# Hybrid decoder layer: a transfer rate of 295 GB/s in the list scheduler, and one kind of FFN weight sum stored whole

## The chip, the cores and the metric

One Trainium2 chip, of which the program uses one core: TensorE (PE), VectorE (DVE), ScalarE (ACT), GpSimd (POOL), SyncE (SP), and 16 DMA engines. The metric is the device time of one execution in microseconds (us). Every transfer of the kernel is issued on SP's queue.

## The reference, cut to what matters

One step of a decoder layer for a prompt of 2048 tokens and 8 decoding tokens, D_MODEL = 1024, all in float32: a mixer (a convolution module beside a gated DeltaNet, one output projection), cross-attention into 256 memory tokens, and a SwiGLU FFN with D_FF = 2816, each behind an RMSNorm and with a residual. The part that the change touches:

```
def swiglu(h, w_gate, w_up, w_down):
    return (jax.nn.silu(h @ w_gate) * (h @ w_up)) @ w_down
```

## The kernel before, in words

The tokens are worked in four blocks of 512 (b = 0 to 3). The mixer runs over two pairs of blocks first (about 0 to 740 us for the projections, on to some 1200 us with the first two attentions); then come FFN 0, attention 2, FFN 1, attention 3, FFN 2, FFN 3. The 8 decoding tokens ride along.

**Weights.** TensorE multiplies float32 data as two parts. A weight tile of 128 x 512 float32 (256 KB) is loaded into a raw tile (`rpool`, 11 of them, `NRAW`) and split into a tile `w` (`wpool`, 6 slots, `NW`): ScalarE copies it, rounded, into the first half, and GpSimd or VectorE writes raw minus that half into the second (`WS.split`, lines 951 to 975). A product then takes three matmuls for each 128 x 128 piece: high by high, high by low, low by high (`three`).

**FFN with sums.** Gate and up projections of one f (128 of the 2816 columns, 22 f in all) are computed by a scheme of Winograd's kind: seven products in place of eight, on blocks of half the rows and half the tokens (`ffn`, `product`). Three of the products take a plain half of w_gate or w_up (Q1, Q2, P4), four take a sum of such halves: P5, P6, Q3 and Q7, which are kinds 0 to 3 (`PROD`, line 803). Kind 3 is gate half 0 plus up half 0. The sums of f = 0 to 7 are made late in the mixer's second pair (`SUMS_AT`, about 490 to 740 us), those of f = 8 to 21 in FFN 0. Each sum is added into a raw tile, split into a w slot like any weight, and that slot, both halves, 512 KB, is stored to the DRAM tensor `sums`, 22 x 4 stores (line 972). For f = 0 to 7 the split slot is used for nothing else; for f = 8 to 21 it also feeds FFN 0's product. All other uses load the 512 KB from `sums` straight into a w slot, without a raw tile (line 957): 8 x 4 in FFN 0 and 22 x 4 in each of FFN 1 to 3, 296 loads.

**Order of the weights.** `Plan` (line 726 on) is the list of all weight tiles in the order of use. An entry either names a raw tile (a load, a sum of two raws) or, with -1, a direct load into w. `WS.pump` loads and splits ahead in that order: raws up to 4 entries ahead (8 in an FFN) and while one of the 11 raw tiles is free, splits while one of the 6 slots is free.

**Order of the instructions.** Two models of time decide it. First, while the program is generated, class `Clock` with `dma` (lines 600 to 608, 360 bytes per ns) decides which lane of work goes on next; this gives the program's order. Second, `Tape` records every operation and `Tape.order` lists them anew for all five engines: it takes a cost for each (`Tape.cost`), and lets the operation go next whose engine and inputs are free first, by a key from the program's order. A transfer costs SP 450 ns; its data start 1100 ns after the issue or when the transfers before it have ended, take size / 360 ns (line 190), and count as there 0.91 to 0.985 us later, according to the engine that reads them (`LAT`):

```
if e == "sp":
    clock[e] = s + 450
    dma_at = max(dma_at, s + 1100) + ns
    fin = dma_at
```

The engines' queues are then in that order, and each engine takes its own in order, waiting where an input is not there.

Of the kernel before, what the change touches and what calls it, by code (L numbers as in the profile page):

```python
# [8 lines left out]
F32 = mybir.dt.float32  # L9
# [5 lines left out]
P = 128  # L15
# [3 lines left out]
TB = 512  # L19
# [13 lines left out]
NF = DFF // P  # L33
# [69 lines left out]
def elems(ap):  # L103
    n = 1
    for x in ap.shape[1:]:
        n *= x
    return n
# [37 lines left out]
class Tape:  # L145
# [28 lines left out]
    def cost(self, eng, op, args, kw, outs, ins):  # L174

        n = max(elems(a) for a in outs + ins) if ins else elems(outs[0])
        psum_in = any(a.name in self.psum for a in ins)
        if eng == "pe":
            m = elems(args[1])
            n = elems(args[2])  # L180
            if op == "transpose":
                return max(n, m) * 0.835 + 3, False, None
            if args[1].dtype == F32:
                return 2 * (max(max(m, 64) * 0.835, 2 * n * 0.4492) + 3), False, None
            return max(max(m, 64) * 0.835, (n if n >= 256 else 4 * n) * 0.4492) + 3, False, None
        if eng == "sp":
            size = 4
            for x in outs[0].shape:
                size *= x
            return max(size / 360.0, 90.0), False, None  # L190
        if eng == "act":
            ptr = len(ins) - 1
            return 0.834 * n + (50 if psum_in else 94) + 93 * ptr + (92 if "accum_out" in kw else 0), False, SETS.get(kw.get("func"))
        big = sum(a.name not in self.psum and elems(a) > 1 for a in ins)
        if eng == "dve":
            ptr = any(hasattr(kw.get(k), "shape") for k in ("scalar", "scalar1"))
            half = op in ("tensor_copy", "tensor_scalar") and not psum_in
            return 68 + (61 if ptr else 0) + n * (6.2 if op == "reciprocal" else 0.525 if half else 1.042), big > 1, None
        if kw.get("op") == ALU.pow:
            return 280 + 180 * n, True, None  # L200
        if op in ("memset", "affine_select"):
            return 40 + 0.85 * n, False, None
        return 135 + n * (2.14 if op == "tensor_tensor" else 3.4), True, None
# [388 lines left out]
def hybrid_step(ctx: ExitStack, tc: tile.TileContext, i: dict, o: list):  # L592
# [7 lines left out]
    def dma(out, in_, after=0.0):  # L600
        SP.dma_start(out=out, in_=in_)
        n = 4
        for x in out.shape:
            n *= x
        C.at["sp"] = max(C.at["sp"] + 60, C.when([in_]), after)
        C.at["dma"] = max(C.at["dma"], C.at["sp"] + 1100) + max(n / 360.0, 60.0)
        C.ready[out.name] = max(C.ready.get(out.name, 0.0), C.at["dma"] + 1650)
        C.used[in_.name] = max(C.used.get(in_.name, 0.0), C.at["dma"])
# [21 lines left out]
    dram = tape.pool(ctx.enter_context(tc.tile_pool(name="dram", bufs=1, space=bass.MemoryType.DRAM)), 1)  # L630
# [4 lines left out]
    def nm(s):  # L635
        uid[0] += 1
        return f"{s}_{uid[0]}"
# [114 lines left out]
    plan = Plan()  # L752
# [49 lines left out]

    PROD = {"P5": 0, "P6": 1, "Q3": 2, "Q7": 3}

    def ffn_key(st, f):
        if st in PROD:
            return ("sums", "c", f, PROD[st])
        w, half = {"Q1": ("w_gate", 0), "Q2": ("w_gate", 1), "P4": ("w_up", 1)}[st]
        return (w, "c", f, half)

    def ffn_plan(b):
        at = {}
        for st, f, *j in ffn_steps(b):
            if st == "down":
                plan.append(("w_down", "d", f, j[0]))
            elif st == "dec":
                plan.append((f, "r", j[0] % KC, j[0] // KC * TB))
            elif b or any(f in fs for fs in SUMS_AT.values()):
                plan.append(ffn_key(st, f), -1 if st in PROD else None)
            else:  # L820
                if st == "Q1":
                    plan.append(ffn_key(st, f))
                    at["Q1", f] = plan.raw_of[-1]
                    continue
                if st == "P5":
                    u1, u0 = (plan.raw("dma", "w_up", "c", f, half) for half in (1, 0))
                    g0, g1 = at["Q1", f], plan.raw("dma", "w_gate", "c", f, 1)
                    s1 = plan.raw("sum", u0, u1, f, 0)
                    s2 = plan.raw("sum", s1, g0, f, 1)
                    at = {**at, "Q2": g1, "P4": u1, "P5": s1, "P6": s2}  # L830
                    at["Q3"] = plan.raw("sum", g1, s2, f, 2)
                    at["Q7"] = plan.raw("sum", g0, u0, f, 3)
                plan.append(ffn_key(st, f), at[st])
# [22 lines left out]
    for pair in PAIRS:  # L856
        for st in STEPS:
            k = int(st[1])
# [28 lines left out]
    for b in range(NB):  # L887
        ffn_plan(b)
        if b + 2 < NB:
            out_plan(b + 2)  # L890
            att_plan(b + 2)
        elif b + 1 < NB:
            plan.extend(("w_down", "d", g, j) for g in range(NG - HOLD, NG) for j in range(KC // 2))
    plan.extend(("w_down", "d", NG - 1, j) for j in range(KC // 2))

    wsrc = dict(i)

    class WS:
# [28 lines left out]
        def load(self):  # L927
            j = self.ld
            how, *what = plan.raws[j]
            r = rpool.tile([P, TB], F32, tag="raw", name=nm("raw"))  # L930
            fr = self.done.get(j - NRAW, 0.0)
            if how == "sum":
                x, y, f, k = what
                self.engine(2600.0).tensor_tensor(out=r, in0=self.raw[x], in1=self.raw[y], op=ALU.add)
                self.used(x)
                self.used(y)
            else:
                w, kind, a, b_ = what
                src = wsrc[w]
                if kind in "cd":  # L940
                    dma(r, src[a, b_], fr)
                elif kind == "q":
                    k0 = b_[0]
                    src = src[0, k0 * P : (k0 + 4) * P, a * P : (a + 1) * P].rearrange("(k p) c -> p k c", p=P)
                    dma(r.rearrange("p (k c) -> p k c", k=4), src, fr)
                else:
                    dma(r, src[0, a * P : (a + 1) * P, b_ : b_ + TB], fr)
            self.raw[j] = r
            self.ld += 1

        def split(self):
            j = self.sp
            k = plan.raw_of[j]
            t = wpool.tile([P, 2, TB], F32R, tag="w", name=nm("w"))
            if k < 0:
                _, _, f, n = plan[j]
                dma(t.bitcast(F32), wsrc["sums"][f, n], self.ends.get(j - NW, 0.0))
                self.tiles[j] = t
                self.sp += 1
                return  # L960
            r = self.raw[k]
            A.activation(out=t[:, 0, :], in_=r, func=AF.Copy)
            if self.pool_lo == "near":
                eng = self.engine()
            elif self.pool_lo is None:
                eng = G if max(C.at["pool"], S.vt) + 600 < max(C.at["dve"], S.vt) else V
            else:
                eng = G if (self.pool_lo or any(c[0] is not None for c in convs)) and j > 9 else V
            eng.tensor_tensor(out=t[:, 1, :], in0=r, in1=t[:, 0, :].bitcast(F32), op=ALU.subtract)
            if plan[j][0] == "sums":  # L970
                _, _, f, n = plan[j]
                dma(wsrc["sums"][f, n], t.bitcast(F32))
            self.tiles[j] = t
            self.sp += 1
            self.used(k)
# [1001 lines left out]
    zd = {(h, b): dram.tile([P, TB], F32, tag=f"z{h}_{b}", name=f"z{h}_{b}") for h in range(H) for b in range(NB)}  # L1977
    udone, cat_done, sdone, zdone = set(), set(), set(), set()
    wsrc["wk"] = dram.tile([1, D, D], F32, tag="wk", name="wk")
    wsrc["sums"] = dram.tile([NF, 4, P, 2, TB], F32, tag="sums", name="sums")  # L1980
    xpark = dram.tile([NB - 1, KC, P, TB], F32, tag="xpark", name="xpark")
    wsrc["vp"] = dram.tile([1, D, D], F32, tag="vp", name="vp")
# [91 lines left out]
    for pair in PAIRS:  # L2074
# [3 lines left out]
        for st in STEPS:  # L2078
# [8 lines left out]
            k = int(st[1])  # L2087
# [342 lines left out]
    def norm_res(xs, done, gain, res, rows_too, split=True):  # L2430

        yield from norm_raw(
            [(lambda k=k: k in done, lambda k=k: xs()[k]) for k in range(KC)], gain, res, True, split, rows_too,
            spare=0,
        )
# [455 lines left out]
```

## Time and profile before

| | |
|---|---|
| runs of the kernel before | 2984.43, 2984.06, 2978.11 us (median 2984.06) |
| the profiled execution, own time | 2980.41 us |
| its span, first to last instruction | 2978.7 us |
| mean granted clock of TensorE | 0.996 |
| PE, DVE, ACT, POOL busy | 98%, 66%, 46%, 50% of the span |
| moved by DMA | 593.89 MB, 199 GB/s on the mean |

Shares are of the span. TensorE's matmuls are pipelined, so that "busy" is time in which at least one is under way. Tiles are named without numbers: `w<-raw` is the split's copy, `w<-raw,w` its subtraction, `w<-sums` a load of a stored sum, `fx`, `fy`, `fz` the banks of the seven products, `dn` those of the down projection. Almost every instruction carries line 469, the line that issues the recorded operations, so groups are told apart by tile names.

### The profile page before, as it was taken

Reading aid. Unit: us, or ns where it says so; the run is one execution under the profiler, and the core shown is the slowest. Engines: PE = TensorE matmul, PEld = TensorE weight load, DVE = VectorE, ACT = ScalarE, POOL = GpSimd, SP = SyncE. Lnnn points to the kernel's source line nnn. Section 1 sums busy time; section 2 is a strip of 40 time slices with the busy share of each in tenths; the row PEclk is TensorE's granted clock in tenths of the full one; section 3 lists DMA queues with packets and bytes.
Section 4 is the critical chain, followed back from the end, with each engine's and each line's share of the span. In section 5 each row is a group of like instructions: output and inputs, shape, how many; then the busy total and the mean of one; then the engine's idle time right before and its main releaser. Section 6 shows DMA issues by size and latency. Waiting matters only on the chain.

```text
span 2978.7 us, 53399 instructions
## 1 busy us (share of the span) xinstructions
PE 2922.9 (98%) x18972; PEld 2601.6 (87%) x18972; DVE 1975.7 (66%) x3973; ACT 1373.8 (46%) x2854; POOL 1478.0 (50%) x1407
## 2 busy tenths in 40 slices
PE   9999999999999998999999999999999999999998
PEld 7999878887888887999988789988888999999997
DVE  8757798987684867957689874433775444664345
ACT  6543556455764545635554553333453232333233
POOL 3544545776656454548875124445503444344444
PEclk9999999999999999999999999999999999999999
DMA  6533435877773435766778767867526666676663
GB/s 213 158 96 106 130 110 163 262 239 255 225 224 112 140 101 162 253 190 222 256 251 273 252 210 244 262 227 241 176 93 233 208 223 214 213 245 216 223 220 134
DMA packets 361962, 593.89 MB, mean 199 GB/s; under 512 B 54016, under 2 KB 148544, under 8 KB 361680
## 3 DMA queue, kind: packets, MB, share of 16 engines
q1 hardware_dynamic: 361696, 590.47, 61.4%
q8 instruction: 151, 2.47, 0.3%
q14 instruction: 115, 0.94, 0.1%
HBM read 476.65 MB, written 114.27 MB: 198 GB/s over the span
## 4 chain that ended last, share of the span: by engine, by line
PE 76%; DVE 7%; issue 5%; DMA 5%; POOL 5%; ACT 2%; SPq 0%; POOLq 0%; DVEq 0%; ACTq 0%
PE dn L469 14%; PE hd L469 11%; PE fy L469 11%; PE rg L469 9%; PE fx L469 7%; PE fz L469 7%; PE sc L469 5%; POOL w L469 3%; DVE cacc L469 3%; PE pu L469 2%; PE glua L469 2%; PE glub L469 2%; DMA w<-sums 1%; PE pch L469 1%; PE po L469 1%
## 5 line engine op out<-in xcount | busy, mean ns | idle before, releaser
L469 POOL TENSOR_TENSOR w<-raw,w 128x512 fp32r<-128x512 f32 x709 | 957.4, 1361 | 877.7 <-ACT w L469 830.3
L469 ACT ACTIVATE w<-raw 128x512 fp32r<-128x512 f32 x912 | 568.6, 631 | 827.7 <-PE fx L469 175.0
L469 PE MATMUL dn<-ff,w 128*128 128x512 f32 (+2 forms) x2688 | 514.2, 347 | 0.8 <-DVE ffs L469 0.6
L469 PEld LDWEIGHTS dn<-ff,w 128*128 128x128 f32 x2688 | 422.8, 188 | 61.5 <-issue 0.8
L469 PE MATMUL fy<-op,w 128*128 128x256 f32 (+1 forms) x3168 | 426.5, 282 | 3.6 <-DMA w<-sums 3.5
L469 PEld LDWEIGHTS fy<-op,w 128*128 128x128 f32 x3168 | 398.6, 188 | 8.9 <-DVE ffu L469 2.8
L469 PE MATMUL hd<-hT,w 128*128 128x512 f32 (+2 forms) x1920 | 397.7, 357 | 8.2 <-ACT w L469 6.0
L469 DVE SCALAR_TENSOR_TENSOR cacc<-cu,cw,cacc 128x512 f32<-128x512 f32 x480 | 359.5, 749 | 16.1 <-ACT cacc L469 8.2
L469 PEld LDWEIGHTS hd<-hT,w 128*128 128x128 f32 x1920 | 304.3, 189 | 52.5 <-ACT w L469 6.8
L469 DVE TENSOR_TENSOR x<-dn,x 128x512 f32<-128x512 f32 (+1 forms) x448 | 254.4, 572 | 139.4 <-PE dn L469 136.1
L469 PE MATMUL fz<-op,w 128*128 128x256 f32 (+1 forms) x2112 | 287.4, 282 | 0.2 <-DMA w<-sums 0.2
L469 PE MATMUL fx<-op,w 128*128 128x256 f32 (+1 forms) x2112 | 284.7, 282 | 0.3
L469 PEld LDWEIGHTS fx<-op,w 128*128 128x128 f32 x2112 | 267.2, 189 | 6.9 <-issue 1.2
L469 PEld LDWEIGHTS fz<-op,w 128*128 128x128 f32 x2112 | 265.3, 188 | 2.2 <-issue 1.3
L469 POOL TENSOR_TENSOR sqj<-sqj,sqj 128x512 f32<-128x512 f32 (+1 forms) x98 | 134.1, 1368 | 265.5 <-ACT sqj L469 263.3
L469 DVE TENSOR_TENSOR w<-raw,w 128x512 fp32r<-128x512 f32 x203 | 180.0, 892 | 69.4 <-ACT w L469 66.0
L469 PE MATMUL rg<-pT,w 128*128 128x512 f32 x768 | 191.5, 401 | 8.1 <-ACT cres L469 7.9
L469 PE MATMUL sc<-w,hT 128*128 128x512 f32 x768 | 189.4, 398 | 2.4 <-DVE w L469 1.3
L469 PE MATMUL rg<-catS,w 128*128 128x512 f32 (+1 forms) x960 | 188.2, 352 | 1.8 <-ACT jn L469 1.7
L469 DVE TENSOR_TENSOR ffu<-fy,ffu 128x256 f32<-128x256 f32 (+1 forms) x176 | 74.4, 423 | 167.2 <-PE fy L469 167.2
L469 PEld LDWEIGHTS rg<-catS,w 128*128 128x128 f32 x960 | 154.4, 188 | 27.0 <-ACT jn L469 2.5
L469 PEld LDWEIGHTS rg<-pT,w 128*128 128x128 f32 x768 | 142.0, 190 | 40.7 <-ACT cres L469 8.3
(378 smaller groups left out, 4101.2 us busy)
## 6 DMA issues: line engine op xcount, KB each, us to landing
w<-sums SPq DMA_DIRECT2D x296, 512.0 KB, 4.5
raw<-in_w_gate_dram SPq DMA_DIRECT2D x192, 256.0 KB, 3.3
sums<-w SPq DMA_DIRECT2D x88, 512.0 KB, 4.1
raw<-in_w_down_dram SPq DMA_DIRECT2D x176, 256.0 KB, 3.0
raw<-in_w_up_dram SPq DMA_DIRECT2D x118, 256.0 KB, 2.9
raw<-in_w_in_dram SPq DMA_DIRECT2D x96, 256.0 KB, 3.1
raw<-in_w_out_dram SPq DMA_DIRECT2D x64, 256.0 KB, 4.3
raw<-wk SPq DMA_DIRECT2D x64, 256.0 KB, 2.9
```

The costliest lines, as they stand in the source:

```text
L469: fn(*args, **kw)
```

## The change

The list scheduler's rate for transfers goes from 360 to 295 GB/s (`Tape.cost` alone; `dma` in line 606 keeps 360). Kind 3 (`WHOLE = (3,)`, product Q7) is kept in a DRAM tensor of its own, `sums1`, as the float32 sum: it is stored from the raw tile, 256 KB, and each later use loads those 256 KB into a raw tile and splits them like a plain weight. Kinds 0 to 2 stay as they are, and so do the additions and first splits of kind 3.

```diff
--- before.py
+++ after.py
@@ -187,7 +187,7 @@
             size = 4
             for x in outs[0].shape:
                 size *= x
-            return max(size / 360.0, 90.0), False, None
+            return max(size / 295.0, 90.0), False, None
         if eng == "act":
             ptr = len(ins) - 1
             return 0.834 * n + (50 if psum_in else 94) + 93 * ptr + (92 if "accum_out" in kw else 0), False, SETS.get(kw.get("func"))
@@ -802,6 +802,9 @@
 
     PROD = {"P5": 0, "P6": 1, "Q3": 2, "Q7": 3}
 
+
+    WHOLE = (3,)
+
     def ffn_key(st, f):
         if st in PROD:
             return ("sums", "c", f, PROD[st])
@@ -816,7 +819,12 @@
             elif st == "dec":
                 plan.append((f, "r", j[0] % KC, j[0] // KC * TB))
             elif b or any(f in fs for fs in SUMS_AT.values()):
-                plan.append(ffn_key(st, f), -1 if st in PROD else None)
+                if st not in PROD:
+                    plan.append(ffn_key(st, f))
+                elif PROD[st] in WHOLE:
+                    plan.append(ffn_key(st, f), plan.raw("dma", "sums1", "u", f, WHOLE.index(PROD[st])))
+                else:
+                    plan.append(ffn_key(st, f), -1)
             else:
                 if st == "Q1":
                     plan.append(ffn_key(st, f))
@@ -937,7 +945,7 @@
             else:
                 w, kind, a, b_ = what
                 src = wsrc[w]
-                if kind in "cd":
+                if kind in "cdu":
                     dma(r, src[a, b_], fr)
                 elif kind == "q":
                     k0 = b_[0]
@@ -967,9 +975,12 @@
             else:
                 eng = G if (self.pool_lo or any(c[0] is not None for c in convs)) and j > 9 else V
             eng.tensor_tensor(out=t[:, 1, :], in0=r, in1=t[:, 0, :].bitcast(F32), op=ALU.subtract)
-            if plan[j][0] == "sums":
+            if plan[j][0] == "sums" and plan.raws[k][0] == "sum":
                 _, _, f, n = plan[j]
-                dma(wsrc["sums"][f, n], t.bitcast(F32))
+                if n in WHOLE:
+                    dma(wsrc["sums1"][f, WHOLE.index(n)], r)
+                else:
+                    dma(wsrc["sums"][f, n], t.bitcast(F32))
             self.tiles[j] = t
             self.sp += 1
             self.used(k)
@@ -1977,6 +1988,7 @@
     zd = {(h, b): dram.tile([P, TB], F32, tag=f"z{h}_{b}", name=f"z{h}_{b}") for h in range(H) for b in range(NB)}
     udone, cat_done, sdone, zdone = set(), set(), set(), set()
     wsrc["wk"] = dram.tile([1, D, D], F32, tag="wk", name="wk")
+    wsrc["sums1"] = dram.tile([NF, len(WHOLE), P, TB], F32, tag="sums1", name="sums1")
     wsrc["sums"] = dram.tile([NF, 4, P, 2, TB], F32, tag="sums", name="sums")
     xpark = dram.tile([NB - 1, KC, P, TB], F32, tag="xpark", name="xpark")
     wsrc["vp"] = dram.tile([1, D, D], F32, tag="vp", name="vp")
```

## Rows read from the trace of the kernel before

**Rows 1.** The page: busy time of each engine, and all DMA traffic.

```profile
PE 2922.9 (98%) x18972; PEld 2601.6 (87%) x18972; DVE 1975.7 (66%) x3973; ACT 1373.8 (46%) x2854; POOL 1478.0 (50%) x1407
...
DMA packets 361962, 593.89 MB, mean 199 GB/s; under 512 B 54016, under 2 KB 148544, under 8 KB 361680
```

**Rows 2.** Windows by stage: length, each engine's busy us (instructions), clock, DMA share, GB/s.

```profile
540.00:740.00 200.00, 197.76 (x989) 161.21 (x988) 168.32 (x291) 109.23 (x218) 147.84 (x146) 0.99 0.79 258
740.00:1200.00 460.00, 438.71 (x2568) 374.26 (x2566) 333.86 (x647) 247.96 (x564) 249.50 (x242) 0.99 0.53 164
...
1380.00:1620.00 240.00, 238.86 (x1628) 215.72 (x1627) 188.70 (x278) 123.54 (x252) 187.52 (x145) 1.00 0.75 254
...
1740.00:2100.00 360.00, 357.13 (x2440) 325.34 (x2439) 164.19 (x290) 132.00 (x249) 162.94 (x124) 1.00 0.76 248
...
2640.00:2960.00 320.00, 319.39 (x2239) 298.13 (x2238) 133.99 (x235) 101.05 (x196) 141.97 (x107) 1.00 0.65 212
```

**Rows 3.** Who PE waited for, whole span: us in total, times, longest us.

```profile
PE rg L469 <- ACT cres L469: 7.9, 1, 7.9
...
PE vp L469 <- ACT jn L469: 3.8, 4, 2.0
PE fy L469 <- DMA w<-sums: 3.5, 6, 1.0
...
PE pu L469 <- DMA Tm<-zt: 2.9, 2, 2.0
PE hd L469 <- POOL w L469: 2.2, 1, 2.2
PE lnp L469 <- DMA lnx<-cvT: 2.1, 1, 2.1
PE wk L469 <- ACT jn L469: 1.9, 1, 1.9
...
PE fz L469 <- DMA w<-sums: 0.2, 1, 0.2
```

**Rows 4.** The page: DMA issues, count, KB each, median us from issue to landing.

```profile
w<-sums SPq DMA_DIRECT2D x296, 512.0 KB, 4.5
raw<-in_w_gate_dram SPq DMA_DIRECT2D x192, 256.0 KB, 3.3
sums<-w SPq DMA_DIRECT2D x88, 512.0 KB, 4.1
```

**Rows 5.** Groups, 1740 to 2960 us, POOL, then ACT: busy us, mean ns, idle before.

```profile
L469 POOL TENSOR_TENSOR w<-raw,w 128x512 fp32r<-128x512 f32 x339 | 458.0, 1364 | 547.5 <-ACT w L469 512.1 <-DMA w<-sums 24.8 <-DMA out_dram<-x 2.8
...
L469 ACT ACTIVATE w<-raw 128x512 fp32r<-128x512 f32 x397 | 248.8, 630 | 424.6 <-PE fx L469 155.4 <-PE fy L469 76.6 <-PE fz L469 62.7
```

**Rows 6.** Windows of 10 us inside 540 to 740 us, columns as in rows 2.

```profile
560.00:570.00 10.00, 10.00 (x56) 8.47 (x55) 10.00 (x17) 7.00 (x15) 7.23 (x8) 1.00 0.93 326
570.00:580.00 10.00, 10.00 (x50) 7.96 (x48) 8.10 (x15) 3.71 (x7) 8.14 (x10) 1.00 1.03 329
...
670.00:680.00 10.00, 10.00 (x47) 8.15 (x46) 8.12 (x21) 4.24 (x7) 6.91 (x11) 1.00 1.04 375
690.00:700.00 10.00, 7.76 (x39) 6.20 (x38) 9.75 (x16) 3.62 (x8) 6.53 (x6) 0.99 0.99 331
```

**Rows 7.** DMA issues, whole span: a store of 256 KB, columns as in rows 4.

```profile
xpark<-x SPq DMA_DIRECT2D x24, 256.0 KB, 3.8
```

**Rows 8.** Who SP's queue waited for, 1380 to 1620 us, columns as in rows 3.

```profile
SPq L469 <- POOL w L469: 55.1, 38, 6.8
SPq L469 <- DVE w L469: 26.0, 20, 3.9
...
SPq L469 <- POOL raw L469: 11.7, 9, 3.2
```

**Rows 9.** Who PE waited for, 1380 to 1620 us: all of it.

```profile
PE pu L469 <- DMA Tm<-zt: 0.9, 1, 0.9
PE dn L469 <- ACT ffs L469: 0.2, 1, 0.2
```

## The prediction

> **What bounds the kernel now.** I read the page's busy time first: TensorE is busy 2922.9 of 2978.7 us, so whatever the change does to the other engines, only 55.8 us of TensorE idle can be won [rows 1]. The same rows give the bytes moved, 593.89 MB. Next the stages, as windows: the idle of TensorE (window minus PE busy) is 2.2 us in the crowded mixer stretch 540 to 740, 21.3 us in 740 to 1200, 1.1 us in 1380 to 1620 (second half of the first FFN block, where sums are made), 2.9 us in 1740 to 2100 (second block) and 0.6 us in 2640 to 2960 (last block) [rows 2]. The reader is to see that the stages that carry the sums are nearly full of matmuls, and that the idle sits in the mixer's second half, which reads no sums at all. Third, who ends TensorE's waits: the sums' loads end 3.5 + 0.2 us of them in seven waits, none over 1.0 us; two other transfers 2.9 and 2.1 us; tiles that go out to DRAM and come back as weights (jn) 3.8 and 1.9 us; a weight split on GpSimd 2.2 us; and one stop of 7.9 us belongs to an ACT instruction [rows 3]. So the kernel is bound by TensorE, and the change is worth what it does to a few short waits and to the order in which every engine's instructions stand.
>
> **Part one, kind 3 kept whole.** There are 296 loads and 88 stores of 512 KB, a quarter of each of kind 3: 74 loads and 22 stores become 256 KB [rows 4]. That is 96 x 0.262 = 25.2 MB less, 4.2% of all traffic [rows 1]. In 1740 to 2100 it is 22 x 0.262 = 5.8 MB of 89. Such a load is now sent for a raw tile (11 of them, loaded ahead) and not for a slot of w.
>
> What it is worth: 0.262 MB at that stage's 248 GB/s is 1.06 us [rows 2]. A sums load that follows one of kind 3 in the transfers' queue lands sooner by up to this, and the longest of the waits to be removed is 1.0 us [rows 3]. I take all of them: 3.7 us. The bounds are 3.7 us gained, and 3.7 us more where the extra raw loads stand in SP's queue ahead of a sums load and wait for a raw tile.
>
> What it adds: 74 copies on ScalarE at 630 ns = 46.6 us and 74 subtractions, on GpSimd at 1364 ns = 100.9 us [rows 5]. In a block of 22 that is 14 and 30 us; in 1740 to 2100 ScalarE is busy 132 and GpSimd 163 of 360 us [rows 2], so both have room and I cost this at nothing. The work that hides it is the matmuls of the other five slots of w. The new wait is ScalarE's, for a slot that TensorE frees; behind it in its queue stand the copies and Silu of the product banks, which TensorE needs back. From the free slot to a ready weight it takes 0.63 + 1.36 = 2.0 us, against 4.5 us for the transfer it replaces [rows 4, 5], so the weight is not late. Without that cover each of 74 uses could hold TensorE for up to 2.0 us, 148 us; the slots' present 397 splits do not, since no wait on them shows in the FFN [rows 3], so I do not carry this into the range.
>
> The eight f of the mixer stage still split kind 3, though nothing reads that split; its slot no longer waits for a store. The eight additions and splits there stay as they are: no time.
>
> **Part two, 295 in place of 360.** It moves no byte. It changes the reckoned end of every transfer, so the order that the list writes out for all five engines, SP's and GpSimd's queues too. A transfer is reckoned at 1.1 us to start, its bytes, and 0.93 us until TensorE may use it: for 256 KB 1.1 + 0.73 + 0.93 = 2.76 us before and 2.92 after, for 512 KB 3.49 before and 3.81 after. Measured medians from issue to landing are 3.3 and 4.5 us [rows 4]. So the list believed transfers 0.54 and 1.0 us early, and put what reads them too early into in-order queues; the change mends 0.16 and 0.32 us, about a third of either.
>
> What it acts on: the two waits on other transfers (5.0 us), those behind weights that were written and read back (5.7 us) and the split behind crowded transfers (2.2 us), together 12.9 us [rows 3]. Bounds: all of it gone, 12.9 us; with the 7.9 us stop gone as well, which is an accident of order in ScalarE's queue, 20.8 us; on the other side a rewritten list can put as much of it elsewhere, so 12.9 us more, since no row excludes that. I take the third that the mended part stands for, 4.3 us, nearest to the landings, which are the only rows that measure the reckoned quantity.
>
> The Trainium skill ("DMA: Bandwidth & Descriptors", section "Where 436 GB/s comes from") speaks against this part: it puts the limit between HBM and SBUF at about 358 GB/s for a core. By that the old figure was the right one. The trace agrees for bursts: where the engines are full they moved 329 and 375 GB/s in 10 us [rows 6]. It does not for a single transfer, whose landing is nearer to the new figure [rows 4]. By the rule, part two would bring nothing, or the loss in rival two.
>
> **Sum.** -3.7 - 4.3 = -8.0 us against the profiled execution's 2980.4 us (span 2978.7 and 1.7 around it): 2972.4. The median of the runs shown is 3.7 us above that execution, so 2976.1; I say 2976.
>
> **Rivals.** *One: hidden anyway.* The sums' waits are seven in a span of 2979 us, the last block loses 0.6 us in all [rows 2, 3], and program order itself still comes from the old 360, since the second clock (line 606) keeps it; 0.16 us on a transfer then moves few neighbours. In this the change hardly does what it says, as only order that the transfers decide can move. For it: FFN stages already full. Against: 21.3 us of idle in 740 to 1200, which a new order must touch [rows 2]. Time: 2984 less at most 3.7, between 2980 and 2987.
>
> *Two: the old rate was right.* Where transfers really run at over 295 GB/s, the list now reckons its transfer queue fuller than it is and sets readers late. In the mixer stretch four windows of 10 us exceed it, at 326, 329, 375 and 331 GB/s [rows 6]: reckoned at 295 their bytes take 1.05, 1.15, 2.71 and 1.22 us longer, 6.1 us. If all of this reaches TensorE and nothing is won, 2990. It decides where such a reader is alone in TensorE's queue; against it stands that these stages have other matmuls to put in front.
>
> *Three, slower: the raw tiles in the first FFN block.* There kind 3 of 14 f is stored from its raw tile, which until now came free after copy and subtraction, 2.0 us [rows 5]. It will be held by a 256 KB store; such a store lands in 3.8 us [rows 7]. That is 1.8 us longer for 14 tiles, 25 us. SP there already waits for raw tiles: 55.1, 26.0 and 11.7 us on splits and sums in 1380 to 1620 [rows 8], so later tiles mean later loads, and behind them in SP's queue stand the decode rows' weights and w_down. For a loss: GpSimd is busy 187.5 of 240 us there [rows 2]. Against: TensorE waits for nothing but 1.1 us in it [rows 9], so the loads are ahead by some unknown measure. It decides when that lead is under 1.8 us; half of the price, 12 us, gives 2996.
>
> **How the numbers follow.** A difference of 0.2%, 6 us, is about what a measurement of this kernel can tell from none. Forecast with its better neighbours (the 7.9 us stop gone as well: 2968, all bounds together: 2960): 0.45, its own range 2958 to 2978. Rival one 0.32. Rival two 0.09, rival three 0.14, both slower. So faster 0.45, same 0.32, slower 0.23. The range goes from the bounds of the forecast, 24.5 us gained at the most (2959.6), with 3 us for the spread of runs, to rival three at half price: 2957 to 2996.
>
> **What would show it.** Right in part one: 222 loads and 66 stores of sums at 512 KB, 74 loads of the new tensor, 569 MB in all, and no wait on sums above some tenths of a us in 1740 to 2100. Right in part two: the waits on Tm, lnx and jn shorter by a third in 740 to 1380 and no new one of their size. Rival three would show as TensorE waits on a split between 1380 and 1620, rival two as idle in 540 to 740 above 2.2 us. The forecast is wrong if TensorE's idle stays within 3 us of 55.8, or if a new stop of the kind of the 7.9 us one opens: a rewritten order can make one anywhere, and no row of the old order tells where.

## The result, and the profile after

The changed kernel is faster: 2963.71 us against 2984.16, medians of four runs each, ratio 0.9932 (95% interval 0.9915 to 0.9949). A second measurement beside the experiments gave 0.9930 (0.9910 to 0.9950). The forecast had 2976, and 8 us where 20 were gained. The profiled execution took 2965.75 us, 14.7 us less than the one of before.

The page of the changed kernel, the lines that answer to [rows 1], then the three groups that carry the splits (columns as in [rows 5]):

```profile
PE 2926.8 (99%) x18972; PEld 2605.1 (88%) x18972; DVE 1969.6 (66%) x3978; ACT 1413.4 (48%) x2925; POOL 1581.4 (53%) x1476
...
DMA packets 361963, 568.72 MB, mean 192 GB/s; under 512 B 54016, under 2 KB 148544, under 8 KB 361680
...
L469 POOL TENSOR_TENSOR w<-raw,w 128x512 fp32r<-128x512 f32 x778 | 1053.4, 1364 | 813.7 <-ACT w L469 754.9
L469 ACT ACTIVATE w<-raw 128x512 fp32r<-128x512 f32 x986 | 613.3, 631 | 832.6 <-PE dn L469 177.3
...
L469 DVE TENSOR_TENSOR w<-raw,w 128x512 fp32r<-128x512 f32 x208 | 182.3, 882 | 75.0 <-ACT w L469 73.4
```

Idle of TensorE fell from 55.8 to 2964.0 - 2926.8 = 37.2 us, 18.6 us less; the span fell by 14.7 only, because the same matmuls were busy for 3.9 us longer, in an execution whose mean granted clock was 0.994 where that of before had 0.996. The traffic is 25.2 MB less, as reckoned. The subtractions were 709 on GpSimd and 203 on VectorE, and are 74 more in all, mostly on GpSimd, at the same 1364 ns.

DMA issues of the changed kernel (columns as in [rows 4]): 74 loads and 22 stores of 256 KB have taken the place of as many of 512 KB.

```profile
w<-sums SPq DMA_DIRECT2D x222, 512.0 KB, 4.4
...
sums<-w SPq DMA_DIRECT2D x66, 512.0 KB, 3.7
...
raw<-sums SPq DMA_DIRECT2D x74, 256.0 KB, 2.8
...
sums<-raw SPq DMA_DIRECT2D x22, 256.0 KB, 3.7
```

Who TensorE waited for in the changed kernel (whole span; total, times, longest), the lines to hold against [rows 3]:

```profile
PE hd L469 <- ACT w L469: 6.3, 2, 5.7
...
PE pu L469 <- DMA Tm<-zt: 1.9, 3, 0.9
...
PE vp L469 <- ACT jn L469: 0.7, 1, 0.7
...
PE fz L469 <- DMA w<-sums: 0.2, 1, 0.2
```

The largest one left is mostly the start's (5.7 of 6.3 us). The waits on sums went from 3.7 to 0.2 us, and no row names ACT cres any more, on which TensorE stood for 7.9 us. Windows of the changed kernel (columns as in [rows 2]) say where idle went:

```profile
540.00:740.00 200.00, 197.27 (x1004) 160.45 (x1003) 176.62 (x315) 112.09 (x221) 152.36 (x151) 1.00 0.76 246
740.00:1200.00 460.00, 453.13 (x2662) 389.44 (x2662) 305.70 (x611) 255.36 (x587) 253.13 (x241) 0.99 0.54 170
...
1380.00:1620.00 240.00, 238.26 (x1584) 212.28 (x1584) 190.43 (x276) 121.25 (x249) 182.66 (x139) 1.00 0.71 241
...
1740.00:2100.00 360.00, 358.86 (x2475) 329.46 (x2475) 172.91 (x289) 146.54 (x275) 198.84 (x148) 1.00 0.72 232
```

In 740 to 1200 it is 6.9 us where it was 21.3 [rows 2]. No matmul in it uses a sum until FFN 0 begins (at 1189.7 us before and 1175.3 us after); to say that the stretch reads no sums, as the prediction did, goes too far, since seven of their loads are issued in its last 22 us in the kernel before. The last block was as good as full before.

**Three stages.** Windows at fixed times mix stages that have moved, so I cut the span at two matmuls instead: the first of attention 0's output product of the mixer (`rg<-catS,w`) and the same of attention 2. Work that moves between an attention and FFN 0 stays within one stage this way. For the kernel before these are the first starts in two windows of that tile, 740 to 1300 and 1400 to 1800 us:

```profile
L469 PE MATMUL rg<-catS,w x576: 277/284/496, 850.4 to 1078.8; 128*128 128x256 f32 x64, 128*128 128x264 f32 x64, 128*128 128x512 f32 x64
...
L469 PE MATMUL rg<-catS,w x192: 388/392/481, 1611.2 to 1656.7; 128*128 128x512 f32 x192
```

So: 850.4 us to attention 0 (mixer, memory weights), 760.8 to attention 2 (attentions 0 and 1, FFN 0), 1367.5 for the rest (attentions 2 and 3, FFN 1 to 3). In the changed kernel 852.1, 751.1 and 1360.8: +1.7, -9.7, -6.7. The middle one is itself a difference: up to FFN 0's first product it fell from 339.3 to 323.2 us, and FFN 0 grew from 421.5 to 427.9 us, with TensorE idle for 7.0 us of it where it was 4.7 (before, then changed; columns as in [rows 2]):

```profile
1189.70:1611.20 421.50, 416.79 (x2977) 382.14 (x2976) 320.11 (x568) 218.17 (x485) 288.39 (x253) 1.00 0.73 240
```

```profile
1175.30:1603.20 427.90, 420.88 (x2981) 384.33 (x2980) 339.77 (x602) 224.66 (x500) 311.16 (x274) 0.99 0.68 226
```

Two gains of different kinds, then, and the runs below show that neither comes, in the main, from the part to which the prediction gave it.

### The profile page after: what moved, and what is told of

Its sections match the earlier page's. It is cut to its first block, busy times and chain, and to the rows that moved or that the text cites. A ratio compares the mean times of both kernels' runs of the same rounds, so it can differ in the third digit from the quotient of the medians.

```text
span 2964.0 us, 53559 instructions
## 1 busy us (share of the span) xinstructions
PE 2926.8 (99%) x18972; PEld 2605.1 (88%) x18972; DVE 1969.6 (66%) x3978; ACT 1413.4 (48%) x2925; POOL 1581.4 (53%) x1476
## 4 chain that ended last, share of the span: by engine, by line
PE 81%; DVE 7%; DMA 5%; POOL 3%; issue 2%; ACT 1%; SPq 0%; POOLq 0%; DVEq 0%; ACTq 0%
PE dn L469 16%; PE fy L469 12%; PE hd L469 10%; PE fz L469 8%; PE fx L469 8%; PE rg L469 7%; PE sc L469 5%; PE glua L469 2%; PE pu L469 2%; PE glub L469 2%; DVE cacc L469 1%; PE pch L469 1%; PE mkv L469 1%; POOL w L469 1%; PE po L469 1%
## 5 line engine op out<-in xcount | busy, mean ns | idle before, releaser
L469 POOL TENSOR_TENSOR w<-raw,w 128x512 fp32r<-128x512 f32 x778 | 1053.4, 1364 | 813.7 <-ACT w L469 754.9
L469 ACT ACTIVATE w<-raw 128x512 fp32r<-128x512 f32 x986 | 613.3, 631 | 832.6 <-PE dn L469 177.3
L469 PE MATMUL rg<-catS,w 128*128 128x512 f32 (+2 forms) x960 | 188.2, 352 | 0.0
L469 PEld LDWEIGHTS sc<-w,hT 128*128 128x128 f32 x768 | 141.5, 188 | 34.6 <-DVE w L469 1.4
```

Of the source, the lines that this page charges most:

```text
L469: fn(*args, **kw)
```

## The experiments

All profiles in one table, us; the ratio is to the kernel before, run beside it. "Sums" is TensorE's wait on loads of sums as the profile lists it, "P3" the time from attention 1's first `rg<-pT,w` to FFN 0's first `fx<-op,w`, its output product, all worked out from the first starts in each trace. "Program order" is the order in which the first clock has the operations recorded; kernels with the same word share it:

```
kernel             program  list   ratio   interval         to att 0  to att 2  rest    P3    sums
                   order    rate
before             old      360    1                        850.4     760.8     1367.5  59.8  3.7
rate 362           old      362    1.0045  1.0026 - 1.0064  864.0     764.0     1373.1  60.0  6.3
start 1640         old      360    0.9978  0.9968 - 0.9987  841.1     764.2     1363.8  59.8  2.4
rate 330           old      330    0.9982  0.9970 - 0.9993  851.5     760.7     1362.5  59.8  2.1
rate 295 alone     old      295    0.9963  0.9953 - 0.9973  852.3     762.2     1360.0  59.8  1.1
kind 3 alone       new      360    0.9980  0.9970 - 0.9989  857.3     749.2     1366.6  50.3  1.5
kind 3, rate 300   new      300    0.9965  0.9952 - 0.9978  853.3     759.0     1362.5  50.1  1.6
the change         new      295    0.9932  0.9915 - 0.9949  852.1     751.1     1360.8  50.1  0.2
the change again   new      295    0.9930  0.9910 - 0.9950  851.3     750.4     1360.2  50.1  1.2
kind 3, rate 290   new      290    0.9937  0.9918 - 0.9957  848.4     751.4     1361.7  50.2  0.0
kind 3, rate 270   new      270    0.9998  0.9987 - 1.0008  859.0     758.3     1360.5  50.1  0.0
kinds 0 and 3      third    295    1.0018  1.0007 - 1.0028  860.0     761.1     1360.2  52.4  0.0
room for cres      fourth   360    1.0022  1.0008 - 1.0035  849.4     767.4     1366.1  51.3  2.5
first clock 295    fifth    360    1.0087  1.0066 - 1.0108  883.4     756.9     1368.3  52.6  5.2
```

One profile is one execution, and those of the rate alone, of rate 300, of rate 362 and of first clock 295 were 6, 9, 11 and 6 us above the medians of their kernels; the two of the change agree within 1 us in each stage.

**The two parts apart.** The rate alone:

```diff
-            return max(size / 360.0, 90.0), False, None
+            return max(size / 295.0, 90.0), False, None
```

> The rate 295 alone, all four kinds of sums still stored split. Theory A (the rate mends the order, kind 3 mends the sums' waits, the two add up): the stretch from the first matmul of attention 0 to the first of FFN 0 falls from 339.3 us to about 323 as in the changed kernel, the sums' waits stay near 3.7 us, FFN 0 stays at 421 us and does not grow to 428; time about 2968 us. Theory B (the order is a draw: any new figure deals the stops out anew): no relation to 323 us; time anywhere from 2965 to 3000 us. Theory C (kind 3 alone brought it): 2984 us, the stop of 7.9 us still there.

2970.05 against 2981.25 us. Its waits on TensorE:

```profile
PE rg L469 <- ACT cres L469: 7.9, 1, 7.9
PE vp L469 <- ACT jn L469: 6.0, 6, 2.1
...
PE wk L469 <- ACT jn L469: 4.6, 3, 2.2
...
PE lnp L469 <- DMA lnx<-cvT: 2.0, 1, 2.0
...
PE pu L469 <- DMA Tm<-zt: 1.4, 2, 1.2
...
PE fy L469 <- DMA w<-sums: 0.8, 1, 0.8
...
PE fz L469 <- DMA w<-sums: 0.3, 1, 0.3
```

The time came out as theory A had it, and its reasons did not: the stop is still there, to the tenth of a us, and the waits on sums, which A left to kind 3, are down from 3.7 to 1.1 us without it. From attention 0 to FFN 0 it took 339.1 us and not 323. The gain that the stages show is in the rest, 7.5 us; 2.6 us of it are the waits on sums, and what the others are no run parts. Kind 3 alone, the changed kernel with 360:

```diff
-            return max(size / 295.0, 90.0), False, None
+            return max(size / 360.0, 90.0), False, None
```

> Kind 3 stored whole, rate still 360. Theory A: the sums' waits fall from 3.7 us to under 1, FFN 1 to 3 are 4 to 5 us shorter, the stop of 7.9 us near 1153 us stays, FFN 0 may grow by up to 6 us; time 2978 to 2986 us. Theory B: 2965 to 3000 us, with the large stops at other places. Theory C: about 2964 us.

2975.25 us: below A's band of 2978 to 2986 and inside B's, and by stages again the wrong way round for A. No row of its waits names cres; attention 0 to attention 2 is 11.6 us shorter, the rest only 0.9. The rest in windows, for the kernel before, the rate alone and kind 3 alone (columns as in [rows 2]):

```profile
1611.20:2978.70 1367.50, 1348.64 (x9169) 1235.88 (x9168) 741.24 (x1554) 507.57 (x977) 534.85 (x404) 1.00 0.66 214
```

```profile
1614.50:2974.50 1360.00, 1346.32 (x9169) 1235.18 (x9167) 742.24 (x1554) 507.47 (x976) 536.94 (x404) 1.00 0.67 215
```

```profile
1606.50:2973.15 1366.65, 1350.42 (x9169) 1237.71 (x9167) 753.53 (x1561) 544.95 (x1043) 618.28 (x463) 0.99 0.63 201
```

By TensorE's idle time kind 3 alone does a little more than the 0.9 us say: 18.9 us before, 16.2 with it, 13.7 with the rate alone. Its matmuls were busy for longer in this one execution, at a granted clock of 0.99. Theory C falls with this as well. The two ratios, 0.9963 and 0.9980, multiply to 0.9943; with an interval of 0.0010 to either side on each that reaches the 0.9930 and 0.9932 of both together.

**What the stop was.** TensorE and ScalarE of the kernel before, in order of time:

```profile
1139.12 6.51 PE L469 MATMUL rg<-pT,w 128*128 128x512 f32 x27
1153.52 3.78 PE L469 MATMUL rg<-pT,w 128*128 128x512 f32 x8 [7.89 <-ACT cres L469]
```

```profile
1148.55 1.30 ACT L469 ACTIVATE op<-tt 128x512 fp32r<-128x512 f32 x2 [0.37 <-DVE tt L469]
1151.69 0.42 ACT L469 ACTIVATE op<-xn 128x256 fp32r<-128x256 f32 x1 [1.84 <-DVE xn L469]
1152.36 0.63 ACT L469 ACTIVATE op<-xn 128x512 fp32r<-128x512 f32 x1 [0.25 <-DVE xn L469]
1152.89 0.58 ACT L469 ACTIVATE cres<-cacc 128x512 f32<-128x512 f32 x1
```

Attention 1's output product needs four accumulator banks. In the list of the kernel before three of them get their matmuls in turn, and the fourth comes after them alone, in the bank in which the convolution accumulated (`cacc`). That bank is emptied by the copy `cres<-cacc`, and TensorE goes on 0.05 us after that copy's end. The stop costs more than its 7.9 us: in it the granted clock fell to 0.50, 1.2 GHz, from 1150.4 us on, and it was full again at 1157.2 us, when TensorE was back at work. The window of that stretch (columns as in [rows 2]):

```profile
1150.40:1157.20 6.80, 3.68 (x9) 2.90 (x10) 6.60 (x14) 5.26 (x13) 0.08 (x1) 0.50 0.75 223
```

So eight matmuls behind the stop took 3.78 us, where nine of the same kind in the changed kernel, below, took 2.33. In ScalarE's queue twelve operand copies of FFN 0 (`op`) stand directly ahead of it from 1138.6 us on, and they wait for VectorE in turn. In the changed kernel all four banks get their matmuls in turn, and none of them is the convolution's: that one is emptied earlier and taken at once for the next channels, while the product's matmuls run.

```profile
1131.89 0.60 ACT L469 ACTIVATE cres<-cacc 128x512 f32<-128x512 f32 x1
...
1134.12 0.81 ACT L469 ACTIVATE cacc<-cu,vcol,cw 128x512 f32<-128x512 f32 x1
```

```profile
1136.04 5.79 PE L469 MATMUL rg<-pT,w 128*128 128x512 f32 x24
1141.66 0.60 PE L469 MATMUL pod<-ident,osc 128*128 128x128 f32 x4
1142.02 2.33 PE L469 MATMUL rg<-pT,w 128*128 128x512 f32 x9
```

Which bank a product takes and how early the copy is called is settled in the program's order, by the first clock. Kind 3 changes that order, since its entries now take raw tiles; the list's rate does not, and every kernel of the table with the old program order has P3 at 59.8 to 60.0 us, whatever its rate. Two kernels tried it without kind 3. First, the copy asks for less room, in the second pair of blocks:

```diff
-        yield ("t2", 1 + RES)
+        yield ("t2", 1 + (RES if b < 2 else 0))
         res = t2("cres")
```

> The kernel before; the copy that empties the convolution's accumulator bank asks for one free tile in place of six, in the second pair of blocks, so that it stands earlier in the program's order. No byte and no rate changes. Theory D (the 7.9 us stop is a bank: the fourth accumulator of attention 1's output product takes the convolution's bank, which that copy frees from behind a dozen FFN-norm copies in ScalarE's queue; kind 3 removed it only by another program order): the stop is gone and the last product of attention 1 falls from 59.6 us to about 50, time about 2971 us (8 to 12 us less). Theory E (the stop went with the transfers of kind 3): the stop stays, 2981 us.

P3 fell to 51.3 us and the stop went, so D holds on its place. On its time it does not: 1.0022. The new order opened another stop of the same length in FFN 0, a small DeltaNet matmul behind ScalarE's `lny`:

```profile
PE pu L469 <- ACT lny L469: 7.9, 1, 7.9
```

Second, another program order with no other edit:

```diff
-        C.at["dma"] = max(C.at["dma"], C.at["sp"] + 1100) + max(n / 360.0, 60.0)
+        C.at["dma"] = max(C.at["dma"], C.at["sp"] + 1100) + max(n / 295.0, 60.0)
```

> The kernel before with 295 in place of 360 in the first clock alone (line 606), so another program order with the same bytes and the old list rate. Theory D: its four accumulators stand together in the list, so no stop of 7.9 us, and the last product of attention 1 takes about 50 us; the sums' waits stay at 3 to 4 us; other stops move by some us either way, time 2965 to 2980 us. Theory E: the stop stays.

P3 52.6 us, no stop on cres, and yet 0.87% slower, outside what D allowed: 33 us more before attention 0. So the bytes of kind 3 were not what took the stop away (E falls), and a program order that avoids it can cost more elsewhere.

**Is the rate's gain in its truth?** Other rates, and another start, with either program order.

```diff
-            return max(size / 360.0, 90.0), False, None
+            return max(size / 362.0, 90.0), False, None
```

> The kernel before with a list rate of 362 in place of 360, nearly nothing. Theory A: within 3 us of the kernel before. Theory B: differs by more than 4 us, one way or the other; its stops at other places.

Half a percent in the rate cost 0.45%, 9.4 us by the medians. Its profile, itself 11 us above its median, loses 13.6 us before attention 0: 7.6 us of idle, and 6.0 us in which TensorE was busy for longer at a granted clock of 0.99 in place of 1.00. Waits of that kernel, whole span:

```profile
PE lnq L469 <- DVE lnx L469: 9.0, 3, 4.2
PE rg L469 <- ACT cres L469: 7.9, 1, 7.9
...
PE fy L469 <- DMA w<-sums: 5.7, 6, 2.2
```

That is theory B: in the mixer, where many chains share the engines' queues, a new list can deal the stops anew.

```diff
-                dma_at = max(dma_at, s + 1100) + ns
+                dma_at = max(dma_at, s + 1640) + ns
```

> The kernel before, list rate 360, but a transfer's data reckoned to start 1640 ns after its issue in place of 1100, which mends the whole 0.54 us by which a 256 KB landing was reckoned short. Theory A (truer landings make a better order): at least as good as 295 alone, 2970 us or less. Theory B (any new order deals the stops anew): no relation, 2968 to 2992 us.

0.9978, 2973.17 us: short of A's bound and inside B's, with waits on sums of 2.4 us. By the landings that the prediction took, it mends that of a 256 KB transfer wholly and that of a 512 KB one by half, and is worth rather less than the rate 295, which mends a third of both (0.9963; the intervals just overlap).

```diff
-            return max(size / 360.0, 90.0), False, None
+            return max(size / 330.0, 90.0), False, None
```

> The kernel before with a list rate of 330. Theory A (a truer rate is a better order throughout): between the runs at 360 and at 295, 2972 to 2981 us. Theory B (in the mixer the order is a draw): mixer and first attention differ from both by 5 us or more, 2965 to 2995 us. Theory F (B for the mixer, but in FFN 1 to 3 a slower rate takes the sums' waits away for good): FFN 1 to 3 between 1069 and 1075 us with waits on sums of 1 to 4 us, whatever the mixer does; last product of attention 1 at 59.8 us in all three, since the program's order is the old one.

2974.69 us; by its total A and F are alike, by stages F's figures came true: FFN 1 to 3 (FFN 1 from its first `fx<-op,w` to attention 3, FFN 2 and 3 from theirs to the end) took 1071.9 us where the kernel before took 1075.0, waits on sums 2.1, P3 59.8. B's did not: to attention 0 and from there to FFN 0 this kernel is within 1.4 us of both its neighbours, 360 and 295. So not every new list deals the mixer anew; 362 did. With kind 3 whole, and so the new program order, 300, 290 and 270 in place of 295, and the change itself once more:

```diff
-            return max(size / 295.0, 90.0), False, None
+            return max(size / 300.0, 90.0), False, None
```

> The changed kernel with 300 in place of 295. Theory A: a rate 1.7% off is as good, within 4 us of the changed kernel, 2960 to 2968 us, no stop over 4 us on TensorE before the tail. Theory B: another order, differing by 6 us or more one way or the other, with stops that neither kernel had.

> The changed kernel with 290 in place of 295. Theory A: within 4 us of the changed kernel, 2960 to 2968 us. Theory B: differs by 6 us or more from the changed kernel or from the run at 300.

> The changed kernel with a list rate of 270, slower than any 60 us stretch of the trace moved on the mean but two. Theory A (an optimum near the true landing): slower than at 295 by 3 to 10 us. Theory F: FFN 1 to 3 as at 295 within 2 us, no waits on sums; mixer and FFN 0 drawn anew, 2955 to 2980 us.

> The changed kernel once more, as the base of the runs beside it. Every theory: 0.990 to 0.996 of the kernel before; the last product of attention 1 at 50 us, sums' waits under 0.5 us.

The change again: 2961.04 us, as expected in ratio and P3, with 1.2 us of waits on sums where under 0.5 was expected. 300 gave 2967.58 us and 0.9965, against 0.9930 and 0.9932 for 295. By the ratios, each with its own runs of before, that is some 10 us, by the medians 4 to 7. Its median lies inside A's band and its profile has no stop over 4 us but the start's, as A had it; too little to settle it. 290 is as good as 295 (2962.35 us). 270 loses all that was gained (2980.91 us), and not in the rest, where it is as good as any (1360.5), as F had it: it loses 7 to 8 us in each of the two stages before. A's sign was right there, its place wrong, and its 3 to 10 us too small for the 20 between the medians.

**More of kind 3's kind.**

```diff
-    WHOLE = (3,)
+    WHOLE = (0, 3)
```

> The changed kernel with kinds 0 and 3 whole: another 25 MB less and another 74 splits. If transfers still bound anything, FFN 1 to 3 gain again, 3 us or more. Theory F: nothing is left to gain, as waits on sums are 0.2 us; FFN 1 to 3 within 2 us of the changed kernel's 1070 us, FFN 0 longer by some us where GpSimd and VectorE are fullest, mixer drawn anew; 2960 to 2980 us.

2986.02 us, 0.8% slower than the changed kernel, more than F gave. The rest is unchanged at 1360.2 us with no wait on sums at all, so fewer bytes buy nothing more there; FFN 0 takes 439.0 us in place of 427.9, and its stops are new ones on ScalarE and VectorE:

```profile
PE pqk L469 <- ACT lny L469: 4.0, 1, 4.0
...
PE fz L469 <- DVE ffu L469: 3.7, 1, 3.7
```

Not tried: the traffic of the changed kernel with the program order of before. A kernel that differs in its transfers has another `Plan`, and so another order; the two can't be parted by leaving something out.

## Why the prediction was right or wrong

**Right: the sign, the room, the bytes.** TensorE bounds the kernel, the gain came out of its idle time (55.8 to 37.2 us), and no wait of TensorE's on a split in FFN 0 is longer than 0.4 us in either profile of the change. Rival three's place stayed full: in 1380 to 1620 TensorE is idle 1.7 us, of which one wait of 0.3 us is on a split. FFN 0 as a whole is 6.4 us longer all the same, but most of its new waits are on DeltaNet tiles, and with 290, which has the same splits, it took 422.5 us: this is order again, as far as these runs tell. Rival two's stretch, 540 to 740, is idle 2.7 us where it was 2.2, not the 8 that it priced.

**Wrong: the term of part one.** The step said "I take all of them: 3.7 us", as the saving of fewer bytes. The waits do go (0.2 us, 1.2 in the second profile), but kind 3 is not needed for it: the rate alone takes them to 1.1 us and the rest of the span down by 7.5 us; kind 3 alone takes them to 1.5 and the rest down by 0.9 (2.7 us of idle). Across the table the rest is 1360 to 1363 us for every list rate of 330 or less and 1364 to 1373 for 360 and 362, with either program order. So the term belongs in the main to part two, and the stage gains about 7 us and not 3.7.

**Wrong: the term of part two.** "I take the third that the mended part stands for, 4.3 us" laid the rate's gain on waits in the mixer and counted the 7.9 us stop as an accident of ScalarE's order that the rate might take along. Those waits (on `Tm`, `lnx`, `jn` and one split), 12.9 us before, are 14.0 us with the rate alone, 4.2 with kind 3 alone, and 2.6 and 6.2 in the two profiles of the change, where others came in their place (`lnq` 2.5, `po` and `pch` 1.9 us each in the first): they went with kind 3 and not with the rate. The landing of 3.3 us, from which the third was worked out, is that of w_gate's loads alone; other groups of 256 KB loads have medians from 2.9 to 4.6 us in the kernel before. The rate leaves the 7.9 us stop where it is, too; kind 3 removes it, P3 59.8 to 50.1 us, 9.7 us with the slow matmuls behind it. The step that failed is a sentence in rival one, that program order "itself still comes from the old 360" (line 606, the first clock): true of the rate and false of the change, since giving kind 3 raw tiles lets the first clock load and split at other moments. I costed part one by its bytes and instructions and not by the order that it gives to others.

**Sum.** The two terms were 3.7 and 4.3 us; they measure 6.7 (rest) and 9.7 (to attention 2), with 1.7 back before attention 0, 14.7 us in the profiles and 17 to 20 in the medians. That the middle stage and P3 both give 9.7 is chance, since the stage is 16.1 us won and 6.4 lost. The Trainium skill's limit of about 358 GB/s ("DMA: Bandwidth & Descriptors", "Where 436 GB/s comes from") would have left the rate without a gain; measured, 295 alone is 0.9963. One of the two bursts in which the prediction saw it borne out, 375 GB/s in 10 us, lies above it. The later start, which leaves the list's rate at 360, shortened the rest as well, to 1363.8 us; so I take it that what counts in this list is when a transfer's data may be read, and not the rate of the engines when full, but no run shows this apart.

**By luck.** 362 in place of 360 moves the time by 0.45%, as much as most of the edits here. The 8 us of the forecast stand inside that scatter, and its range of 39 us was about right for that reason and no better one. That the two stages' gains met in one kernel at 295 and 290, and not at 300 or 270, I can't derive from any row of before.

## What to carry to other kernels

Where a program lists its own instructions by a model of time, an edit acts through the order at least as much as through its work: try figures just beside the old one first, to learn how far the time moves for nothing, and believe a gain where it repeats in one stage over many orders, as the rest's 5 to 7 us and the 9.7 us of P3 do. Look up for each large wait which buffer it is that comes late, and which instruction frees it. And part a change of two edits on the chip before explaining it: here the total added up, while each gain came mostly from the other half.

## What the runs showed that was not expected

The same stop of 7.9 us, to the tenth, stood in five kernels with five different lists, though it came between 1150 and 1172 us. That fits a wait that is set by a chain in two other queues and does not feel the transfers around it; the chain itself was followed in the kernel before alone. With kinds 0 and 3 whole, GpSimd is busy 185.6 of the 300 us from 2640 to 2940, where it was 131.4 before, and TensorE, which the kernel before left idle for 0.6 us of that stretch, has no idle time in it at all:

```profile
2640.00:2940.00 300.00, 300.00 (x2124) 281.28 (x2123) 130.20 (x220) 116.97 (x219) 185.60 (x138) 1.00 0.65 195
```
